# Gate and up products of a two-layer transformer trunk: high and low token parts in one 512-column matmul

## Chip, core and metric

The kernel runs on one core of one Trainium2 chip. The metric is the time of one execution on the device, in microseconds (us); less is better. Compared are medians of several runs.

## What is computed

Two layers over 256 tokens of width 1024. Each layer has a feed-forward part (swiglu), a mixer (two kinds of attention side by side) and a second feed-forward part, each between two RMS norms, with shifts, scales and gates worked out from a vector c. Cut to the part that matters here:

```python
D_MODEL, SEQ, DEPTH = 1024, 256, 2
D_FF = 2816

def swiglu(h, w_gate, w_up, w_down):
    return (jax.nn.silu(h @ w_gate) * (h @ w_up)) @ w_down

for l in range(DEPTH):
    mod = (c_act @ ada_w[l] + ada_b[l])[:, None, :]
    sh1, sc1, g1, sh2, sc2, g2, sh3, sc3, g3 = jnp.split(mod, N_MOD, axis=-1)
    h = rmsnorm(x, norm_pre[l, 0]) * (1.0 + sc1) + sh1
    y = swiglu(h, ffn_w_gate[l, 0], ffn_w_up[l, 0], ffn_w_down[l, 0])
    x = x + 0.5 * g1 * rmsnorm(y, norm_post[l, 0])
    ...  # the mixer, then the second swiglu with sh3, sc3, g3
```

All inputs and outputs are float32.

## The kernel before

**Precision.** TensorE multiplies in float32r, a form of float32 that keeps fewer bits. Every weight and every activation is therefore split into a high and a low part (`hi`, `lo`; for the tokens `hTh`, `hTl`), and a product is the sum of three matmuls: high by high, high by low, low by high. For weights ACT writes the high part (line 442) and DVE subtracts it from the raw data to get the low part (line 443), in pieces of 512 or 256 columns (function `unit`, `split` in the table SEC). A weight block is 128 x 2048 elements, 1 MB.

**The feed-forward part** (`ffn`, four calls). Its 2816 hidden columns are taken in 512 columns for each half of the tokens (`rows_of`, weights as the moving operand), and nine blocks of 256 columns (`j` = 0 to 8) for all 256 tokens at once, with the weights as the stationary operand. In a block, gate and up each have two column groups (`t`) of 128 hidden columns. A group is a sum over 8 steps of the inner dimension; `mm3t` runs its three matmuls (lines 489 to 491), each with 256 moving columns, the tokens of both halves. Gate fills one PSUM bank (two groups of 256), up another: `pair = (wps(), wps())`. Then `swiglu` (lines 634 to 638) takes Silu of the gate on ACT (636) and its product with up on DVE (637), both from PSUM; `split` writes the high and the low part of the result (630, 631). These activations are the stationary operand of the down products (`mm3`, lines 481 to 483, 512 columns), which add into four banks over the whole call. `mm3t` is also used in the mixer, in `cols_of` (line 726).

**Tiles and buffers.** `wps` gives a PSUM bank, of two pools (`w0`, `w1`) with two banks each; without an argument the pool goes by the block's parity. The other four banks hold the down sums. `st` gives SBUF tiles of 128 x 512 of two pools with three each. Raw weights have 3 buffers, high parts 6, low parts 5. So a weight load on SP's queue (line 431) waits until DVE has made the low part of an older block.

**Background work.** The shifts and scales of later parts are computed beside: SP loads pieces of `ada_w` (line 514), DVE multiplies and adds them (line 506, `acc`), and two matmuls (523, 524) sum over the partitions.

**The order of the work** is not that of the code. `keep_order` collects all instructions, takes a cost for each, runs a list schedule forward and backward five times, with due times, buffers and the constants of SEC, and fixes the resulting order on every engine. Any change in the instructions makes a new order everywhere.

Of the kernel before, what the change touches and what calls it, by code (L numbers as in the profile page):

```python
# [11 lines left out]
F32R = mybir.dt.float32r  # L12
# [283 lines left out]
def trunk(ctx, tc, x, c, rel_bias, ada_w, ada_b, norm_pre, norm_post, w_gate, w_up,  # L296
# [48 lines left out]
    def wps(h=None):  # L345
        return psw.tile([P, 512], F32, tag=f"w{cur[0] if h is None else h}", name=nm("w"))
# [7 lines left out]
    def ctile(shape, name, dt=F32):  # L354
        return cp.tile(shape, dt, tag=name, name=name)
# [104 lines left out]
    def u_both(l, f, w, tag, j):  # L460

        c0 = 512 + j * 256
        return unit((tag, l, f, "j", j), (8, 256), rows(w[l, f], 0, 8)[:, :, c0:c0 + 256])
# [14 lines left out]
    def mm3(ps_, hh, hl, wt, wk, sl, start, stop):  # L478
# [3 lines left out]
        nc.tensor.matmul(ps_, hh, wl, start=False, stop=False)  # L482
        nc.tensor.matmul(ps_, hl, wh, start=False, stop=stop)  # L483

    def mm3t(ps_, kt, wt, sl, start, stop):

        wh, wl = wt[0][:, kt, sl], wt[1][:, kt, sl]
        hh, hl = hT[0][:, :, kt, :], hT[1][:, :, kt, :]
        nc.tensor.matmul(ps_, wh, hh, start=start, stop=False)  # L489
        nc.tensor.matmul(ps_, wh, hl, start=False, stop=False)  # L490
        nc.tensor.matmul(ps_, wl, hh, start=False, stop=stop)  # L491
# [87 lines left out]
        nc.gpsimd.tensor_tensor(r2, r, mhalf, op=ALU.pow)  # L579
        return r2  # L580

    hT = [ctile([P, 2, KT, P], f"hT{n}", F32R) for n in "hl"]

    def to_T(h, k0, nk, src):

# [70 lines left out]
    def ffn(l, i, first):  # L656
        f = i // 2
        acts = []
        for h in range(2):
            cur[0] = h  # L660
            pair = first[h] if first else (wps(), wps())
            if not first:
                rows_of(h, pair, [lambda q: u_solo(l, f, w_gate, "g", q), lambda q: u_solo(l, f, w_up, "u", q)])
            acts.append(hidden_solo(pair))
        accs = [(aps(h), aps(h)) for h in range(2)]
        blocks = [[(acts[h], t * P) for t in range(4)] for h in range(2)]

        def down(h, u):

            w = u_down(l, f, u)  # L670
            for n in range(2):
                for k in range(2):
                    (hh, hl), c0 = blocks[h][u * 2 + k]
                    mm3(accs[h][n], hh[:, c0:c0 + P], hl[:, c0:c0 + P], w, k, slice(n * 512, (n + 1) * 512),
                        u == 0 and k == 0, u == 10 and k == 1)

        nd = 0
        for j in range(9):
            cur[0] = j % 2
            if first and j == SETUP:  # L680
                with shift(START_SMALL):
                    setup_table(*small)
                setup_bias()
            pair = (wps(), wps())
            for p_, (tag, ws) in zip(pair, (("g", w_gate), ("u", w_up))):
                w = u_both(l, f, ws, tag, j)
                for t in range(2):
                    for k in range(KT):
                        mm3t(p_[:, t * 256:(t + 1) * 256], k, w, slice(t * P, (t + 1) * P), k == 0, k == KT - 1)
            act = split(swiglu(*pair), 512)  # L690
            for h in range(2):
                blocks[h] += [(act, t * 256 + h * P) for t in range(2)]
            while nd < min(j + 2 - sec["lag"], 11 - sec["tail"]):
                for h in range(2):
                    down(h, nd)
                nd += 1
        for h in range(2):
            cur[0] = h
            for u in range(nd, 11):
                down(h, u)  # L700
            post_norm(h, l, i, accs[h])
            if (l, i) != (DEPTH - 1, 2):
                pre_norm(h, *((l, 1) if i == 0 else (l + 1, 0)))
# [340 lines left out]
```

## Time and profile before

| | |
|---|---|
| median of 3 runs | 1026.07 us (1024.99 to 1028.37) |
| the profiled execution | 1029.76 us, its span 1027.6 us |
| PE busy | 1007.1 us (98%), 6514 matmuls and as many weight loads |
| DVE busy | 800.6 us (78%) |
| ACT busy | 552.9 us (54%) |
| mean granted TensorE clock | 0.996 |
| moved by DMA | 265.10 MB |

PE is TensorE with its matmuls, PEld its weight loads, DVE is VectorE, ACT is ScalarE, SP issues the DMAs. The span is the time from the first to the last instruction. A matmul's duration is longer than the distance to the next one, since they are pipelined; the distance between two starts tells what one costs. In the names of tiles `_a` and `_b` stand for the parity of the block (or the half of the tokens), and the arrow points from what is read to what is written.

### The profile page before, as it was taken

The page shows a single profiled execution, that of the slowest core. Times are in us where ns is not written, and L with a number is a line of the kernel's source. Part 1 is how long each engine was busy: PE and PEld are TensorE (multiplying, and loading weights), DVE is VectorE, ACT ScalarE, POOL GpSimd, SP SyncE. Part 2 cuts the span into 40 slices and gives each one's busy share as a digit, 9 for nine tenths or more (in the row PEclk, how much of TensorE's full clock was granted, in tenths as well). Part 3 has the DMA queues.
Part 4 walks back from the last instruction along what each step waited for, and adds up shares of the span by engine and source line. Part 5 has one row for each costly group of instructions (what it writes and reads, how often), then busy time and mean ns, then how long its engine had stood idle before and what let it go on. Part 6 is the DMA issues. An engine that isn't in the chain of part 4 may idle for free. (4 is left out here: it accounts for less than half of the span.)

```text
span 1027.6 us, 17311 instructions
## 1 busy us (share of the span) xinstructions
PE 1007.1 (98%) x6514; PEld 895.9 (87%) x6514; DVE 800.6 (78%) x1493; ACT 552.9 (54%) x1250; POOL 41.3 (4%) x80
## 2 busy tenths in 40 slices
PE   8999998999999999999999999999999999999997
PEld 3699998988897899999979999998788879999996
DVE  4799886988997998798879887886879788555542
ACT  2456433574877665555465544545478666444431
POOL 1000000010001000000010000000100110000000
PEclk9999999999999999999999999999999999999999
DMA  9999999977895588899838988886589638655511
GB/s 327 364 343 340 315 290 342 331 251 251 308 321 203 196 278 294 280 317 312 282 133 290 319 273 276 301 291 242 160 295 330 207 125 274 200 175 195 183 64 41
DMA packets 173919, 265.10 MB, mean 258 GB/s; under 512 B 6412, under 2 KB 109548, under 8 KB 173836
## 3 DMA queue, kind: packets, MB, share of 16 engines
q1 hardware_dynamic: 173680, 263.93, 75.7%
q8 instruction: 51, 0.84, 0.3%
q14 instruction: 32, 0.26, 0.1%
q10 hardware_dynamic: 156, 0.07, 0.0%
HBM read 262.90 MB, written 4.22 MB: 260 GB/s over the span
## 5 line engine op out<-in xcount | busy, mean ns | idle before, releaser
L443 DVE TENSOR_TENSOR lo_a<-raw_a,hi_a 128x512 fp32r<-128x512 f32 (+1 forms) x540 | 293.6, 593 | 48.5 <-issue 24.2
L442 ACT ACTIVATE hi_a<-raw_a 128x512 fp32r<-128x512 f32 (+1 forms) x540 | 259.2, 547 | 121.2 <-DMA raw_a<-in_ffn_w_up_dram 28.3
L489 PE MATMUL w_a<-hTh,hi_a 128*128 128x256 f32 x768 | 219.6, 286 | 3.4 <-ACT hi_a L442 3.4
L490 PE MATMUL w_a<-hTl,hi_a 128*128 128x256 f32 x768 | 218.5, 285 | 0.0
L491 PE MATMUL w_a<-hTh,lo_a 128*128 128x256 f32 x768 | 217.7, 284 | 0.0
L489 PEld LDWEIGHTS w_a<-hTh,hi_a 128*128 128x128 f32 x768 | 147.7, 193 | 5.0 <-ACT hi_a L442 3.6
L490 PEld LDWEIGHTS w_a<-hTl,hi_a 128*128 128x128 f32 x768 | 147.9, 193 | 1.2 <-issue 0.3
L491 PEld LDWEIGHTS w_a<-hTh,lo_a 128*128 128x128 f32 x768 | 147.7, 192 | 0.4
L490 PE MATMUL w_b<-hTl,hi_b 128*128 128x256 f32 x512 | 144.8, 283 | 0.0
L489 PE MATMUL w_b<-hTh,hi_b 128*128 128x256 f32 x512 | 144.7, 283 | 0.0
L491 PE MATMUL w_b<-hTh,lo_b 128*128 128x256 f32 x512 | 144.6, 283 | 0.0
L443 DVE TENSOR_TENSOR lo_b<-raw_b,hi_b 128x512 fp32r<-128x512 f32 (+1 forms) x224 | 119.8, 589 | 24.6 <-issue 17.1
L442 ACT ACTIVATE hi_b<-raw_b 128x512 fp32r<-128x512 f32 (+1 forms) x224 | 105.3, 544 | 62.4 <-DMA raw_b<-in_ffn_w_up_dram 17.5
L489 PEld LDWEIGHTS w_b<-hTh,hi_b 128*128 128x128 f32 x512 | 98.1, 192 | 1.0
L490 PEld LDWEIGHTS w_b<-hTl,hi_b 128*128 128x128 f32 x512 | 98.1, 192 | 0.9
L491 PEld LDWEIGHTS w_b<-hTh,lo_b 128*128 128x128 f32 x512 | 98.0, 192 | 0.3
L506 DVE SCALAR_TENSOR_TENSOR acc_a<-araw_a,ccol,acc_a 128x512 f32<-128x512 f32 x110 | 82.2, 747 | 12.0 <-DMA araw_a<-in_ada_w_dram 10.6
L482 PE MATMUL a_b<-lo_a,str_a 128*128 128x512 f32 x156 | 60.8, 392 | 0.0
L483 PE MATMUL a_b<-hi_a,str_a 128*128 128x512 f32 x156 | 60.2, 390 | 0.0
L481 PE MATMUL a_b<-hi_a,str_a 128*128 128x512 f32 x156 | 59.7, 391 | 0.0
L506 DVE SCALAR_TENSOR_TENSOR acc_b<-araw_b,ccol,acc_b 128x512 f32<-128x512 f32 x46 | 34.5, 749 | 4.7 <-DMA araw_b<-in_ada_w_dram 3.9
L481 PE MATMUL w_a<-hi_a,hTh 128*128 128x512 f32 (+1 forms) x96 | 36.2, 378 | 0.6 <-DVE hTl L591 0.6
(245 smaller groups left out, 1724.1 us busy)
## 6 DMA issues: line engine op xcount, KB each, us to landing
araw_a<-in_ada_w_dram SPq DMA_DIRECT2D x84, 512.0 KB
raw_a<-in_ffn_w_down_dram SPq DMA_DIRECT2D x30, 1024.0 KB
raw_a<-in_ffn_w_gate_dram SPq DMA_DIRECT2D x26, 1024.0 KB
raw_a<-in_ffn_w_up_dram SPq DMA_DIRECT2D x26, 1024.0 KB
araw_b<-in_ada_w_dram SPq DMA_DIRECT2D x44, 512.0 KB
raw_a<-in_mix_w_in_dram SPq DMA_DIRECT2D x18, 1024.0 KB
raw_b<-in_ffn_w_gate_dram SPq DMA_DIRECT2D x16, 1024.0 KB
raw_b<-in_ffn_w_up_dram SPq DMA_DIRECT2D x16, 1024.0 KB
```

Of the source, the lines that this page charges most:

```text
L442: nc.scalar.activation(hi[:, sl], raw[:, sl], AF.Copy)
L443: nc.vector.tensor_sub(lo[:, sl], raw[:, sl], hi[:, sl].bitcast(F32))
L481: nc.tensor.matmul(ps_, hh, wh, start=start, stop=False)
L482: nc.tensor.matmul(ps_, hh, wl, start=False, stop=False)
L483: nc.tensor.matmul(ps_, hl, wh, start=False, stop=stop)
L489: nc.tensor.matmul(ps_, wh, hh, start=start, stop=False)
L490: nc.tensor.matmul(ps_, wh, hl, start=False, stop=False)
L491: nc.tensor.matmul(ps_, wl, hh, start=False, stop=stop)
L506: nc.vector.scalar_tensor_tensor(acc[:, :n], raw[:, t, :], ccol[:, k:k + 1], b if t == 0 else acc[:, :n], op0=ALU.mult, op1=ALU.add)
```

## The change

High and low part of the tokens now lie in one tile, `hTa[p, half, part, step, token]`. In the nine blocks of each feed-forward call a new function `mm2t` runs two matmuls for each step: the high weights against 512 columns (high part of both halves, then low part of both halves), and the low weights against the 256 columns of the high part. Columns 0 to 255 of the bank get high by high and low by high, columns 256 to 511 get high by low. So a column group fills a bank of its own: gate's two groups take the two banks of pool w0, up's those of w1. After a group ACT copies columns 256 to 511 to SBUF and DVE adds columns 0 to 255 to them. Silu and the product of gate and up then work in SBUF, in place. The mixer keeps `mm3t`. The tables of the planner are as they were.

```diff
+    def mm2t(ps_, k, wt, sl):
+        for kt in range(k):
+            wh, wl = wt[0][:, kt, sl], wt[1][:, kt, sl]
+            both = lambda **f: nc.tensor.matmul(ps_, wh, hTa[:, :, :, kt, :].rearrange("p h n t -> p n h t"), **f)
+            if kt < k - 1:
+                both(start=kt == 0, stop=False)
+            nc.tensor.matmul(ps_[:, :256], wl, hT[0][:, :, kt, :], start=False, stop=False)
+            if kt == k - 1:
+                both(start=kt == 0, stop=True)
...
-    hT = [ctile([P, 2, KT, P], f"hT{n}", F32R) for n in "hl"]
+    hTa = ctile([P, 2, 2, KT, P], "hT", F32R)
+    hT = [hTa[:, :, n] for n in range(2)]
...
-            pair = (wps(), wps())
-            for p_, (tag, ws) in zip(pair, (("g", w_gate), ("u", w_up))):
+            gu = []
+            for b, (tag, ws) in enumerate((("g", w_gate), ("u", w_up))):
                 w = u_both(l, f, ws, tag, j)
+                gu.append(st())
                 for t in range(2):
-                    for k in range(KT):
-                        mm3t(p_[:, t * 256:(t + 1) * 256], k, w, slice(t * P, (t + 1) * P), k == 0, k == KT - 1)
-            act = split(swiglu(*pair), 512)
+                    p_ = wps(b)
+                    mm2t(p_, KT, w, slice(t * P, (t + 1) * P))
+                    dst = gu[b][:, t * 256:(t + 1) * 256]
+                    nc.scalar.activation(dst, p_[:, 256:], AF.Copy)
+                    nc.vector.tensor_add(dst, p_[:, :256], dst)
+            nc.scalar.activation(gu[0], gu[0], AF.Silu)
+            nc.vector.tensor_mul(gu[0], gu[0], gu[1])
+            act = split(gu[0], 512)
```

The new order shows it at three places. The first is PE in the third block of the second feed-forward call, before (lines 489 to 491 are `mm3t`):

```order
L489 MATMUL w_a_4400<-hTh,hi_a_4475 128x256
L490 MATMUL w_a_4400<-hTl,hi_a_4475 128x256
L491 MATMUL w_a_4400<-hTh,lo_a_4476 128x256
L489 MATMUL w_a_4400<-hTh,hi_a_4475 128x256
L490 MATMUL w_a_4400<-hTl,hi_a_4475 128x256
L491 MATMUL w_a_4400<-hTh,lo_a_4476 128x256
```

And PE at the same place after (490 is the wide matmul, 493 the narrow one):

```order
L490 MATMUL w_a_4181<-hT,hi_a_4158 128x512
L493 MATMUL w_a_4181<-hT,lo_a_4159 128x256
L490 MATMUL w_a_4181<-hT,hi_a_4158 128x512
L493 MATMUL w_a_4181<-hT,lo_a_4159 128x256
L490 MATMUL w_a_4181<-hT,hi_a_4158 128x512
```

Three matmuls a step have become two, and the two read the same tile `hT`.

The second place is DVE at that block, before (637 is the product of gate and up, 443 a low part of weights, 506 a background sum):

```order
L443 TENSOR_TENSOR lo_b_4606<-raw_b_4603,hi_b_4605 128x256
L506 SCALAR_TENSOR_TENSOR acc_b_4634<-araw_b_4640,ccol,acc_b_4634 128x512
L506 SCALAR_TENSOR_TENSOR acc_b_4634<-araw_b_4712,ccol,acc_b_4634 128x512 x2
L443 TENSOR_TENSOR lo_b_4695<-raw_b_4692,hi_b_4694 128x256 x8
L637 TENSOR_TENSOR st_a_4546<-st_a_4545,w_a_4400 128x512
```

And DVE there after (707 is the new add, 709 the product, 518 a background sum):

```order
L443 TENSOR_TENSOR lo_b_4419<-raw_b_4416,hi_b_4418 128x256 x3
L707 TENSOR_TENSOR st_a_4180<-w_a_4181,st_a_4180 128x256
L443 TENSOR_TENSOR lo_b_4419<-raw_b_4416,hi_b_4418 128x256 x5
L518 SCALAR_TENSOR_TENSOR acc_b_4126<-araw_a_4239,ccol,acc_b_4126 128x512
L707 TENSOR_TENSOR st_a_4180<-w_a_4200,st_a_4180 128x256
L518 SCALAR_TENSOR_TENSOR acc_b_4126<-araw_a_4308,ccol,acc_b_4126 128x512 x2
L443 TENSOR_TENSOR lo_b_4488<-raw_b_4485,hi_b_4487 128x256 x2
L534 TENSOR_TENSOR ast_b_4359<-acc_b_4126,ast_b_4358 128x512
L707 TENSOR_TENSOR st_a_4243<-w_a_4244,st_a_4243 128x256
L443 TENSOR_TENSOR lo_b_4488<-raw_b_4485,hi_b_4487 128x256 x3
L707 TENSOR_TENSOR st_a_4243<-w_a_4263,st_a_4243 128x256
L709 TENSOR_TENSOR st_a_4180<-st_a_4180,st_a_4243 128x512
```

DVE has four adds in a block now, one for each column group, among the low parts of later weights.

The third place is PE in the first feed-forward call, at its third block, before (481 to 483 are down products):

```order
L482 MATMUL a_b_537<-lo_b_855,str_b_530 128x512
L483 MATMUL a_b_537<-hi_b_854,str_b_531 128x512
L489 MATMUL w_a_903<-hTh,hi_a_907 128x256
L490 MATMUL w_a_903<-hTl,hi_a_907 128x256
L491 MATMUL w_a_903<-hTh,lo_a_908 128x256
```

And there after:

```order
L482 MATMUL a_b_536<-lo_b_810,str_b_529 128x512
L483 MATMUL a_b_536<-hi_b_809,str_b_530 128x512
L490 MATMUL w_a_898<-hT,hi_a_860 128x512
L490 MATMUL w_a_934<-hT,hi_a_919 128x512
L490 MATMUL w_a_953<-hT,hi_a_919 128x512
L493 MATMUL w_a_879<-hT,lo_a_861 128x256
L490 MATMUL w_a_879<-hT,hi_a_860 128x512
L493 MATMUL w_a_879<-hT,lo_a_861 128x256
L490 MATMUL w_a_879<-hT,hi_a_860 128x512
L493 MATMUL w_a_898<-hT,lo_a_861 128x256
```

Where the block ran group by group, its four banks are now opened by single wide matmuls, before the low part of the weights is asked for.

## Rows read from the trace of the kernel before

**Rows 1.** Page, busy time (share, instructions) and 40 slices in tenths

```profile
PE 1007.1 (98%) x6514; PEld 895.9 (87%) x6514; DVE 800.6 (78%) x1493; ACT 552.9 (54%) x1250; POOL 41.3 (4%) x80
...
PEclk9999999999999999999999999999999999999999
```

**Rows 2.** Windows: from:to, length, busy us (instructions), clock, DMA share, GB/s

```profile
45.00:225.00 180.00, 176.61 (x1182) 163.13 (x1181) 155.82 (x246) 91.66 (x175) 1.63 (x4) 0.99 0.96 329
225.00:345.00 120.00, 117.83 (x714) 100.22 (x713) 104.14 (x230) 86.22 (x227) 14.09 (x24) 1.00 0.71 241
350.00:500.00 150.00, 150.00 (x1050) 140.88 (x1049) 132.29 (x308) 87.12 (x252) 0.00 (x0) 1.00 0.87 296
550.00:725.00 175.00, 174.60 (x1194) 162.37 (x1192) 141.21 (x222) 87.51 (x165) 5.06 (x8) 1.00 0.81 278
725.00:835.00 110.00, 107.47 (x648) 90.94 (x648) 92.03 (x199) 74.38 (x189) 9.32 (x16) 1.00 0.73 239
850.00:1000.00 150.00, 150.00 (x1071) 141.93 (x1071) 85.32 (x137) 70.62 (x130) 0.00 (x0) 1.00 0.54 183
...
375.00:400.00 25.00, 25.00 (x153) 22.41 (x152) 23.34 (x55) 13.27 (x41) 0.00 (x0) 1.00 0.90 305
```

**Rows 3.** PE's waits, the longest: us in total, times, longest

```profile
PE w_a L489 <- ACT hi_a L442: 3.4, 1, 3.4
```

**Rows 4.** Timeline of PE, a block product: start, duration, engine, line, operation

```profile
970.90 0.28 PE L489 MATMUL w_b<-hTh,hi_b 128*128 128x256 f32 x1
...
982.29 0.28 PE L491 MATMUL w_b<-hTh,lo_b 128*128 128x256 f32 x1
```

**Rows 5.** Timeline of PE, down products

```profile
505.90 0.40 PE L481 MATMUL a_b<-hi_a,str_b 128*128 128x512 f32 x1
...
522.93 0.39 PE L481 MATMUL a_b<-hi_a,str_b 128*128 128x512 f32 x1
```

**Rows 6.** Page, costliest groups: count, busy us, mean ns, idle before

```profile
L489 PE MATMUL w_a<-hTh,hi_a 128*128 128x256 f32 x768 | 219.6, 286 | 3.4 <-ACT hi_a L442 3.4
L489 PE MATMUL w_b<-hTh,hi_b 128*128 128x256 f32 x512 | 144.7, 283 | 0.0
```

**Rows 7.** Timeline of PE, mixer products with 256 columns in one piece

```profile
229.99 0.28 PE L482 MATMUL w_a<-lo_a,hTh 128*128 128x256 f32 x1
...
232.14 0.28 PE L482 MATMUL w_a<-lo_a,hTh 128*128 128x256 f32 x1
```

**Rows 8.** Groups of DVE and ACT by form, columns as in rows 6

```profile
L968 DVE TENSOR_TENSOR st_a<-st_a,w_a 128x256 f32<-128x256 f32 x4 | 1.7, 421 | 0.1
L637 DVE TENSOR_TENSOR st_a<-st_a,w_a 128x512 f32<-128x512 f32 x23 | 15.7, 685 | 15.7 <-PE w_a L491 14.8 <-PE w_a L483 0.7
L637 DVE TENSOR_TENSOR st_b<-st_b,w_b 128x512 f32<-128x512 f32 x19 | 13.0, 683 | 10.6 <-PE w_b L491 9.7 <-PE w_b L483 0.9
L606 DVE TENSOR_TENSOR st_a<-x,row_a 128x512 f32<-128x512 f32 x6 | 3.9, 685 | 0.0
L506 DVE SCALAR_TENSOR_TENSOR acc_a<-araw_a,ccol,acc_a 128x512 f32<-128x512 f32 x110 | 82.2, 747 | 12.0 <-DMA araw_a<-in_ada_w_dram 10.6
L590 ACT ACTIVATE hTh<-w_a 128x256 fp32r<-128x256 f32 x4 | 1.5, 384 | 12.3 <-PE w_a L588 12.3
```

**Rows 9.** Waits of SP's queue: us in total, times, longest

```profile
SPq L431 <- DVE lo_a L443: 311.4, 102, 13.3
SPq L431 <- DVE lo_b L443: 137.0, 44, 7.1
```

**Rows 10.** Timeline of PE and windows around its long wait

```profile
162.26 0.28 PE L490 MATMUL w_a<-hTl,hi_a 128*128 128x256 f32 x1
165.93 0.39 PE L489 MATMUL w_a<-hTh,hi_a 128*128 128x256 f32 x1 [3.39 <-ACT hi_a L442]
...
162.00:166.00 4.00, 0.61 (x6) 0.41 (x4) 0.09 (x1) 0.76 (x2) 0.00 (x0) 1.00 1.04 403
166.00:175.00 9.00, 9.00 (x63) 9.00 (x64) 8.02 (x13) 5.47 (x11) 0.00 (x0) 0.81 0.98 339
```

## Prediction, made before the changed kernel had run

> **What bounds the kernel now.** I read the page's busy table and slices first [rows 1]. PE is busy 98% of the span, and its clock line reads 9 throughout. DVE comes next with 78%, ACT with 54%. That is a mean over unlike stages, so I then read the window table by stage [rows 2]. The four feed-forward stages (here 45 to 225, 350 to 500, 550 to 725 and 850 to 1000 us) show PE busy 176.61 of 180, 150 of 150, 174.60 of 175 and 150 of 150 us; only the two mixers and the start show PE waiting. A busy PE need not be a PE at its best, so the third view is PE's waits [rows 3]: the longest is one of 3.4 us, for the high part of one weight block. In the feed-forward stages the end is therefore set by how many matmuls PE has to run and how far apart they start.
>
> **What a matmul costs.** In the product of one block, 96 matmuls of 256 columns start between 970.90 and 982.29 us [rows 4]: 11.39 us over 95 steps, 119.9 ns from start to start. The down products run 76 matmuls of 512 columns between 505.90 and 522.93 us [rows 5]: 17.03 us over 75 steps, 227.1 ns. The line through both is 0.419 ns for a column and 12.7 ns for a matmul whatever its width (227.1 - 119.9 = 107.2 ns for 256 more columns; 119.9 - 107.2 = 12.7). Each matmul has its own weight load in both stretches, so the 12.7 ns is for the pair.
>
> **The change part by part.**
> *Products.* Lines 489 to 491 run 768 and 512 times each [rows 6], 1280 times; 2 layers x 4 calls x 2 halves x 8 steps = 128 of these are the mixer's cols_of, which stays. In 1152 steps, three matmuls of 256 columns (3 x 119.9 = 359.7 ns) become one of 512 and one of 256 (227.1 + 119.9 = 347.0 ns). The step loses 12.7 ns and one weight load; 1152 x 12.7 ns = 14.6 us, 3.7 us in each of four feed-forward stages. The columns that move through PE stay the same.
>
> *The form of the wide operand.* The 512 columns are four pieces of 128 with two different distances between them, which no matmul of the trace has. Nearest rows: 256 columns in two pieces start 119.9 ns apart [rows 4], and 256 columns in one piece, between 229.99 and 232.14 us, 2.15 us over 18 steps, 119.4 ns [rows 7]. A break costs 0 to 0.5 ns. At the other end, a 512-column matmul that is worth no more than two of 256 would cost 239.8 ns and save nothing. I take 227.1, since the row for breaks is the nearer one; three breaks at 0.5 ns would take 1.7 us of the 14.6.
>
> For the 12.7 ns, the trace and the Trainium skill differ. The Trainium skill (TensorE: Matmul & The Clock Gate, section "Wait — 56ns, not 53.3ns?") puts the fixed part of a warm matmul at about 2.5 ns, measured on bf16; by it the 1152 removed matmuls would be worth an estimated 2.9 us. The rows disagree; they are of this kernel's float32r products, and the sum goes by them.
>
> *Work added behind PE.* Each of the 144 column groups now leaves its bank through an ACT copy and a DVE add of 128x256. The same kinds of instruction stand in the trace: an ACT copy from PSUM of 128x256 with 384 ns, a DVE tensor_tensor of 128x256 with one PSUM operand with 421 ns [rows 8]. The Silu and the product of the gate are as many as before; they read SBUF now, which for a DVE product of 128x512 makes no difference (685 ns at line 606 as at line 637) [rows 8]. So a feed-forward stage gets 36 x 0.384 = 13.8 us of ACT and 36 x 0.421 = 15.2 us of DVE. ACT has room everywhere (87.12 busy of 150 us in the second stage). DVE idles 24.2, 17.7, 33.8 and 64.7 us in the four windows [rows 2]. The second is the tight one: 17.7 us less the 3.7 that the stage gets shorter leaves 14.0 for 15.2. What makes it fit is the order: between the first and the last block product of that stage DVE had 52 of the background sums of line 506 and has 47 now (the first stage 56 and 49, the third 55 and 40), and five of them are 5 x 0.747 = 3.7 us [rows 8]. They go to the stretches between stages; DVE is at 87% and 84% in the mixers' windows. I count this at nothing and give it a rival.
>
> *The wait that is new.* The first wide matmul of a group now waits until the DVE add has emptied the bank's last holder; behind it on PE stands everything. After a group ends the chain is a copy and an add, 0.384 + 0.421 us, and the same bank is wanted only three groups later, 3 x 8 x 347 ns = 8.3 us. Nothing is paid as long as the add is not kept behind other work for over 7 us.
>
> *The tail of a block.* From its last matmul to the split, a block went through Silu and product and now goes through copy, add, Silu and product, 0.8 us more. The down products take their activation a block or more later, and 96 down matmuls (21.8 us at 227.1 ns) follow the last block in both orders. Nothing.
>
> *Order and queues.* The planner orders everything anew. In the first stage it now opens the four banks of a block with single wide matmuls ahead of their low weights; in the last it alternates wide and narrow. The queue of SP has the same 421 rows in a changed order. Weight loads are issued when the low split of an older block frees its buffer: SP's longest waits are for line 443 on DVE, 311.4 and 137.0 us in all [rows 9]. So DVE's lateness travels by the DMA queue to the next weights.
>
> **How much of 14.6 us arrives.** The second, third and fourth stage have PE at 100% and DMA engines at 0.87, 0.81 and 0.54 [rows 2]. I count their 3 x 3.7 = 11.0 us in full. The first has DMA at 0.96 over 180 us, and PE's one long wait lies in it: after 162.26 us the next matmul starts at 165.93, waiting for a high part, with the DMA engines at 1.04 meanwhile, and over the next 9 us the granted clock is 0.81 on average, so part of them went at the lower of its two levels [rows 10]. A PE that arrives there earlier waits longer. I count nothing for the first stage. The mixers I count as they were: their order changes in places, with no sign that I can read.
>
> Sum: -11.0 us. The profiled execution took 1029.76 us, with a span of 1027.6; less 11.0 that is 1018.8 and a span of 1016.6. This execution lay 3.7 us above the median of 1026.07, so the median should be **1015** us.
>
> **The rivals.**
> *All of it and the long wait too.* If the new order brings the block of 162 us in time, the first stage gains its 3.7 us, the gap of 3.6 us closes, and the 9 us at 0.81 give back 1.7: 1026.1 - 14.6 - 3.6 - 1.7 = 1006 us. For it: the gap is one event, and the loads around it are reordered. Against it: DMA at its limit.
>
> *DVE fills up in the second stage.* Then the 3.7 us of that stage go too, and, as the background sums moved between the stages, up to 4 us of the gains there: 1026.1 - 7.3 = 1018.8, with the sums 1023. For it: 14.0 us of room for 15.2 us of adds, and SP waiting for DVE. Against it: windows of 25 us with DVE 93% busy (23.34 of 25) keep PE busy for all 25 [rows 2].
>
> *No gain in the product.* The wide matmul at 239.8 ns, because its four pieces are fetched as two: 1026. A fixed part far below 12.7 ns would come out nearly there. The rule of the Trainium skill named above would give an estimated 1023 to 1024. Against both stand two straight stretches of rows.
>
> *The adds wait at the head of DVE's queue: slower.* The products of line 637 waited for PE 14.8 + 9.7 us [rows 8], over 42 of them 0.58 us each. If each add waits as long, it holds DVE 1.0 us, 36 us in a stage; less the background sums that left (7, 5 and 15 at 0.747 us), DVE is short of 6.6 us in the first stage and 14.6 in the second, has room in the others, and these gain 3.7 each: 21.2 - 7.4 = +13.8, 1040 us. It decides from the point where a wait of an add exceeds (17.7 + 3.7 - 15.2 - 3.7) / 36 = 0.07 us in the second stage and (24.2 + 5.2 - 15.2 - 3.7) / 36 = 0.29 us in the first; slower than before it gets from about 0.4 us. Against it: while DVE waits for PE, PE is the late one, and the low parts behind the add were made some blocks ahead.
>
> **How the numbers follow.** The forecast has 0.50, its own range 1010 to 1019 (the first stage's 3.7 us, the breaks, a little of the mixers). All of it and the wait 0.10, DVE filling up 0.20, no gain 0.08, slower 0.12. The range reaches from 1006 to 1025: it leaves out the slower case and half of no gain. What a measurement can tell from no change is about 0.3%, 3.1 us, so faster means under 1023: 0.50 + 0.10 + 0.20 = 0.80; same 0.08; slower 0.12.
>
> **What would show it.** In the changed profile: 1152 fewer matmuls and weight loads (5362); in a clean block, wide and narrow matmuls starting 227 and 120 ns apart, 347 ns a step (240 and 120 would be the third rival); 144 copies near 0.38 and 144 adds near 0.42 us; DVE over 90% in the second stage with PE still at 100%; the stretch from the first to the last block shorter by some 3.7 us in three stages and not in the first. Wrong would be: waits of PE for low parts in the second stage, DVE adds that wait long for PE while the split behind them is wanted, or mixers that grow by more than 3 us.

## Result and profile after

The changed kernel takes 1035.56 us (median of five runs; the kernel before in the same batch 1028.37): 1.0084 times the time, interval 1.0060 to 1.0107. That is slower, 20 us above the forecast and outside its range. One of the five executions took 1656.43 us at a mean granted clock of 0.557 and is left out of the ratio. The profiled execution took 1039.71 us with a span of 1037.9, against 1029.76 and 1027.6. So the two profiles lie 10 us apart and the medians 7; what is read from the profiles below is to be taken with these 3 us.

The first line of the profile page of the changed kernel (busy us, share, instructions) answers to [rows 1]:

```profile
PE 1003.7 (97%) x5362; PEld 835.5 (81%) x5362; DVE 848.1 (82%) x1637; ACT 599.0 (58%) x1394; POOL 40.8 (4%) x80
```

The 1152 matmuls and weight loads are gone. Yet PE is busy only 3.4 us less, and it is idle 34.2 us (1037.9 - 1003.7) where it was idle 20.5 (1027.6 - 1007.1). The windows of [rows 2], now of the changed kernel, show where:

```profile
45.00:225.00 180.00, 171.94 (x869) 142.58 (x868) 156.85 (x267) 97.83 (x198) 0.82 (x1) 0.98 0.91 306
225.00:345.00 120.00, 115.45 (x694) 97.48 (x693) 103.55 (x223) 84.07 (x221) 12.34 (x22) 0.99 0.77 260
350.00:500.00 150.00, 149.96 (x780) 127.54 (x779) 134.83 (x317) 92.01 (x261) 1.33 (x3) 1.00 0.78 263
550.00:725.00 175.00, 175.00 (x905) 149.09 (x905) 157.75 (x266) 97.03 (x195) 0.83 (x2) 1.00 0.88 301
725.00:835.00 110.00, 105.34 (x651) 89.73 (x650) 91.39 (x199) 73.21 (x188) 9.71 (x17) 1.00 0.75 248
850.00:1000.00 150.00, 149.85 (x784) 127.51 (x783) 106.83 (x183) 86.91 (x171) 1.21 (x2) 1.00 0.60 200
sum 885.00, PE 867.55 PEld 733.93 DVE 751.20 ACT 531.06 POOL 26.24; mean PE 144.59 PEld 122.32 DVE 125.20 ACT 88.51 POOL 4.37
```

PE idles 8.1 us in the first window (3.4 before), 4.6 and 4.7 in the two mixers' windows (2.2 and 2.5), and next to nothing in the other feed-forward stages. PE's longest waits in the changed kernel (us in total, times, longest), where [rows 3] had one of 3.4 us:

```profile
PE a_b L481 <- ACT hi_a L442: 5.9, 2, 5.5
PE w_a L481 <- DVE hT L605: 3.3, 1, 3.3
...
PE w_b L831 <- ACT st_b L825: 2.2, 1, 2.2
PE w_a L736 <- DVE st_a L781: 1.5, 1, 1.5
PE w_b L602 <- DVE st_b L859: 1.3, 1, 1.3
```

None of them is for a copy or an add of the change. L481 is a down product that waits for the high part of its weights, and then, at 541.29 us, the first product of the third feed-forward call, which starts when DVE has written the low part of the first tokens (L605). L831, L736 and L602 belong to the mixers and the norms. The wait at 541.29 shows what an order does:

```profile
537.63 1.07 ACT L604 ACTIVATE hT<-w_a 128x512 fp32r<-128x512 f32 x2
539.22 1.42 DVE L638 SCALAR_TENSOR_TENSOR x<-st_b,rstd_b,x 128x512 f32<-128x512 f32 x2 [0.24 <-POOL rstd_b L591]
540.55 0.68 DVE L605 TENSOR_TENSOR hT<-w_a,hT 128x512 fp32r<-128x512 f32 x1
541.29 0.50 PE L481 MATMUL w_a<-hi_a,hT 128*128 128x512 f32 x1 [3.34 <-DVE hT L605]
```

The high part, all that this product reads, was there at 538.70. DVE did the norm of the other half of the tokens (L638) ahead of L605. Whether PE waited for the joined tile `hT` or for the PSUM bank that L605 still had to read is not told apart; with two separate tiles, before, the same kind of product also waited once for the low part, 0.6 us (at 229.77). The longest wait, in the timeline of PE and of ACT and in windows (columns as in the windows above):

```profile
175.01 0.40 PE L536 MATMUL w_a<-ast_a,onesr 128*128 128x512 f32 x1
180.92 1.22 PE L481 MATMUL a_b<-hi_a,str_a 128*128 128x512 f32 x2 [5.52 <-ACT hi_a L442]
...
180.24 1.67 ACT L442 ACTIVATE hi_a<-raw_a 128x512 fp32r<-128x512 f32 x3 [5.08 <-DMA raw_a<-in_ffn_w_down_dram]
...
175.00:181.00 6.00, 0.48 (x3) 0.08 (x1) 1.39 (x3) 0.93 (x3) 0.00 (x0) 0.91 1.04 361
181.00:200.00 19.00, 19.00 (x86) 15.86 (x87) 14.87 (x25) 11.06 (x23) 0.00 (x0) 0.85 1.06 337
```

It is of the kind of the wait in [rows 10], 13 us later in the span and 2.1 us longer. PE waits for a conversion by ACT, ACT for a DMA, and the DMA engines are full. The granted clock is 0.85 over the 19 us behind it, so part of them went at the lower level.

**A ledger.** Add up, in each trace, what every matmul of the product functions (mm3, mm3t, mm2t) takes from its start to the next one's beyond 119.9 ns (256 columns) or 227.1 ns (512), and all the time of the other matmuls (transposes, attention, sums). Before this is 132.2 us, after it is 157.3. From before to after the last matmul's start moves by 1031.3 - 1021.0 = +10.3 us; that is -14.6 us for the merged matmuls at the forecast's price and +25.1 us of this sum (the rest is rounding). Of the 25.1, some 6 us are a spacing that the forecast had too small (below). The other 19 lie by stage: first feed-forward call 7.0, first mixer 4.4, the transition from the second call to the third 4.2, second mixer 1.6, start 1.6, the rest spread. By the first and last block product of each call, the third call went from 150.4 to 148.0 us and the fourth from 143.1 to 140.7, each 2.4 us shorter. The end of the first call came 3.4 us later; mixer, second call and transition together went from 339.8 to 349.7 us; the second mixer grew by 1.7. The second call itself, with the transition to the third, went from 192.6 to 195.0 us, though the forecast had its 3.7 us in full.

### The profile page after: what moved, and what is told of

The parts are those of the page before. It is cut to its first block, busy times and chain, and to the rows that moved or that the text cites. A ratio compares the mean times of both kernels' runs of the same rounds, so it can differ in the third digit from the quotient of the medians.

```text
span 1037.9 us, 15226 instructions
## 1 busy us (share of the span) xinstructions
PE 1003.7 (97%) x5362; PEld 835.5 (81%) x5362; DVE 848.1 (82%) x1637; ACT 599.0 (58%) x1394; POOL 40.8 (4%) x80
## 5 line engine op out<-in xcount | busy, mean ns | idle before, releaser
L490 PE MATMUL w_a<-hT,hi_a 128*128 128x512 f32 x640 | 223.9, 397 | 0.0
L490 PE MATMUL w_b<-hT,hi_b 128*128 128x512 f32 x512 | 179.4, 397 | 0.0
L493 PE MATMUL w_a<-hT,lo_a 128*128 128x256 f32 x640 | 166.8, 281 | 0.1
L490 PEld LDWEIGHTS w_a<-hT,hi_a 128*128 128x128 f32 x640 | 116.8, 188 | 22.4
L493 PE MATMUL w_b<-hT,lo_b 128*128 128x256 f32 x512 | 132.5, 281 | 0.0
L493 PEld LDWEIGHTS w_a<-hT,lo_a 128*128 128x128 f32 x640 | 120.7, 189 | 7.5 <-DVE lo_a L443 0.6
L490 PEld LDWEIGHTS w_b<-hT,hi_b 128*128 128x128 f32 x512 | 93.5, 188 | 18.1 <-ACT hi_b L442 0.2
L493 PEld LDWEIGHTS w_b<-hT,lo_b 128*128 128x128 f32 x512 | 96.5, 189 | 6.0
L518 DVE SCALAR_TENSOR_TENSOR acc_a<-araw_a,ccol,acc_a 128x512 f32<-128x512 f32 x110 | 82.1, 746 | 14.0 <-DMA araw_a<-in_ada_w_dram 12.7
L481 PE MATMUL a_b<-hi_a,str_a 128*128 128x512 f32 x156 | 60.7, 402 | 5.5 <-ACT hi_a L442 5.5
L707 DVE TENSOR_TENSOR st_a<-w_a,st_a 128x256 f32<-128x256 f32 x80 | 33.3, 420 | 21.7 <-ACT st_a L706 21.5
L481 PE MATMUL w_a<-hi_a,hT 128*128 128x512 f32 (+1 forms) x96 | 37.1, 386 | 3.3 <-DVE hT L605 3.3
L481 PEld LDWEIGHTS a_b<-hi_a,str_a 128*128 128x128 f32 x156 | 30.2, 194 | 11.9 <-ACT hi_a L442 6.0
```

The source lines that it names most:

```text
L481: nc.tensor.matmul(ps_, hh, wh, start=start, stop=False)
L490: both = lambda **f: nc.tensor.matmul(ps_, wh, hTa[:, :, :, kt, :].rearrange("p h n t -> p n h t"), **f)
L493: nc.tensor.matmul(ps_[:, :256], wl, hT[0][:, :, kt, :], start=False, stop=False)
L518: nc.vector.scalar_tensor_tensor(acc[:, :n], raw[:, t, :], ccol[:, k:k + 1], b if t == 0 else acc[:, :n], op0=ALU.mult, op1=ALU.add)
L707: nc.vector.tensor_add(dst, p_[:, :256], dst)
```

## Experiments

Two theories stand against each other. **The order** (O): the matmuls gain, but the planner writes every queue anew, with constants that were chosen for the old instructions, and the new order lets PE wait in stages where it does not set the end. **The added work** (B, and E for the adds alone): copies, adds and the banks that they hold cost the time in any order. A side question (P, Q) is why a step gained less than 12.7 ns. Ratios are to the kernel before in the same batch, with the interval.

**e1: the merge taken back, the rest kept.** Banks, copies and adds as in the change, three matmuls of 256 columns (those of the low token part ahead of the others), the order made anew (arguments shortened):

```
+  for kt in range(k): matmul(ps_[:, 256:], wt[0][:, kt, sl], hT[1][:, :, kt, :])
   for kt in range(k):
-      both(...)
+      matmul(ps_[:, :256], wh, hh)
       matmul(ps_[:, :256], wl, hh)
```

> The changed kernel with its wide matmul taken apart again: banks, copies and adds as changed, but high by low as 256-column matmuls of its own (first the eight of a group, then the pairs), 6514 matmuls. In the changed kernel's trace a wide matmul starts the next after 233 ns and a narrow one after 118, 351 ns a step, against 360 for three narrow ones. Theory O (the product gains, the new order of the work loses it): slower than the changed kernel by 1152 x 9 ns = 10 us, so about 1045 us. Rival P (the wide matmul saves nothing): the same as the changed kernel within 3 us, about 1035.

Measured: 1042.6 us, 1.0134 [1.0110, 1.0158]. That is 7 us above the change (5 by the ratios), nearer to theory O's 1045 than to P's 1035, and 14 us above the kernel before with as many matmuls. The merge gains; the loss is in the rest. The 7 us are not the merge's price alone, since the order is another one too.

**e2: no adds, the planner free.**

```
-  activation(dst, p_[:, 256:], Copy)
-  tensor_add(dst, p_[:, :256], dst)
+  activation(dst, p_[:, :256], Copy)
```

> The changed kernel without the 144 adds on DVE: ACT copies columns 0 to 255 of each bank, and the product of high weights with low tokens, which PE still computes, is left out of the result. Rival E (the adds themselves cost: DVE's 48 to 60 us of work and the waits at the head of its queue): falls by the whole loss, to about 1015. Theory O: the order is made anew without the adds, so some of the loss may go by chance, but PE's idle time in the mixers and the first stage (28 us more than before) stays for the larger part: 1025 to 1035.

Measured: 1023.94 us, 0.9957 [0.9940, 0.9974]. That is between the two forecasts. 11.6 us come back with the adds, but the planner also made another order: both theories can have this.

**e3 and e4: the planner's price of a matmul.** The planner prices a matmul by its columns with a small fixed part; here it gets the line of [rows 4, 5], in the changed kernel (e3) and in the kernel before (e4). No instruction is added or left out.

```
-  return max(free, 256) / 2.4 + 2.5
+  return free * 0.419 + 12.7
```

> The changed kernel, but the planner takes for a float32r matmul what the trace shows, 0.419 ns a column and 12.7 ns a matmul (227 ns for 512 columns, 120 for 256), where it had 216 and 109. Nothing else is changed: the same instructions in another order. Theory O: the idle time comes from the order, so another order moves the time by more than 3 us, and one made with true costs gets most of the gain: 1015 to 1022. Rival E: the work on DVE is the same, so within 4 us of the changed kernel, 1031 to 1039.

> The kernel before with the same true matmul costs in its planner: what another order alone does to it. Theory O in its strong form (the constants of the tables fit the order that before had, and any other order is worse): slower by 3 to 10 us, 1031 to 1038. In the weak form (true costs make a better order for either): 1015 to 1025. Rival E says nothing of it.

Measured: e3 1039.01 us, 1.0100 [1.0073, 1.0126]; e4 1051.2 us, 1.0233 [1.0204, 1.0262]. e3 is a miss for theory O: truer prices made no better order, and the time is at the upper end of rival E's range. Its longest wait of PE is for one of the new adds. The add stands on DVE behind four low parts and a background sum, and holds the bank into which PE is to sum over the partitions (L535). So the change does add waits that an order can run into:

```profile
PE w_b L535 <- DVE st_b L707: 5.1, 2, 4.7
```

e4 is the strongest single result on the order. The kernel before, with the same instructions in another sequence, is 22 us slower, more than the 3 to 10 us that were expected. Windows of e4:

```profile
45.00:225.00 180.00, 170.03 (x1143) 157.03 (x1142) 153.76 (x242) 85.90 (x160) 0.29 (x1) 0.97 0.97 327
225.00:345.00 120.00, 113.76 (x684) 95.96 (x684) 95.82 (x208) 77.75 (x205) 11.26 (x20) 1.00 0.73 241
350.00:500.00 150.00, 146.03 (x943) 133.09 (x942) 129.23 (x300) 86.06 (x249) 2.04 (x4) 0.99 0.82 273
...
725.00:835.00 110.00, 104.67 (x629) 88.79 (x628) 84.21 (x182) 68.38 (x174) 7.66 (x15) 0.98 0.74 238
```

It idles 10.0 us in the first window, 6.2 and 5.3 in the mixers and 4.0 in the second feed-forward stage: mostly the places at which the changed kernel lost, without any of the change.

**e5: small adds in the same order.** The add covers 7 of the 256 columns; the planner prices it as the full one, so that every queue keeps the changed kernel's order.

```
-  tensor_add(dst, p_[:, :256], dst)
+  tensor_add(dst[:, :7], p_[:, :7], dst[:, :7])
```

> The changed kernel with every instruction in its place on every queue (the planner still counts the adds as before), but each of the 144 adds on DVE touches 7 columns in place of 256, so the product of high weights with low tokens is left out of nearly all of the result. The 144 waits of DVE for ACT's copy stay; some 144 x 0.26 = 37 us of DVE work go. Theory O (the order loses the gain): within 4 us of the changed kernel, 1031 to 1037. Rival E (the adds' time on DVE loses it): 1020 to 1026.

Measured: 1035.03 us, 1.0073 [1.0061, 1.0086]. Groups of DVE in e5 (count, busy us, mean ns, idle before):

```profile
L709 DVE TENSOR_TENSOR st_a<-w_a,st_a 128x7 f32<-128x7 f32 x80 | 12.7, 162 | 30.4 <-ACT st_a L708 30.3
L709 DVE TENSOR_TENSOR st_b<-w_b,st_b 128x7 f32<-128x7 f32 x64 | 10.1, 162 | 24.7 <-ACT st_b L708 24.2
```

The adds went from 420 and 419 ns to 162, 37 us less of DVE, and the time by 0.5 us. In this order DVE's time isn't what is paid for.

**e6: the wide operand in one piece.** The wide matmul reads 512 neighbouring columns, all of the high part; the order is the same.

```
-  hTa[:, :, :, kt, :].rearrange("p h n t -> p n h t")
+  fl(hTa[:, 0, 0, 0:4, :])
```

> The changed kernel in the same order on every queue, but the wide matmul reads 512 columns that lie in one piece (the same ones at every step, so the results of the blocks are wrong numbers). In the changed kernel wide matmuls start the next after 233 ns, the down products' after 227. If the four pieces cost the 6 ns: a step of 347 ns, 1152 x 4 to 6 ns = 5 to 7 us faster than the changed kernel where PE is the limit, about 1029 to 1031. If they do not: the same as the changed kernel, 1033 to 1037, and 233 in the trace.

Measured: 1035.78 us, 1.0082 [1.0069, 1.0096]. The breaks in the operand cost nothing.

**e7: the change in the second layer's calls alone** (`if l == 1:` the new block, else the old one).

> The change in the third and the fourth feed-forward call alone; the first two use the old product. In the changed kernel those two stages were each 2.4 us shorter from first to last block matmul, the first was 1.8 us longer and the stretch between first and second 7.4 us longer. Theory O: the third and fourth give 4.8 us, and the order of the first layer is again a new one with chance gains or losses of some us: 1021 to 1030. Rival E: DVE has 34 and 65 us idle in these two stages, the adds fit: about 1024.

Measured: 1027.69 us, 0.9983 [0.9971, 0.9996]. The third and fourth call are 2.3 and 2.4 us shorter, as in the full change. Of these 4.7 us, 0.2 are left by the medians (1027.91 before in this batch) and 1.7 by the ratio. The first mixer, none of whose instructions the edit touches, grew from 147.2 to 151.9 us between the block products around it; PE is busy 114.12 us in its window, where it was 117.83 [rows 2]:

```profile
225.00:345.00 120.00, 114.12 (x692) 96.63 (x691) 100.94 (x222) 81.57 (x218) 11.14 (x21) 1.00 0.72 236
```

**e8: the changed kernel near the old order.** What is ready is ranked by its place in the order of the kernel before, in one pass of the planner:

```
-  best = forward(prio)
-  last = best
-  for _ in range(FBI):
...
+  best = forward(ranks_of_before)
```

> The changed kernel, its matmuls, copies and adds untouched, but the planner ranks what is ready by the place that the instruction had in the order of the kernel before (the wide matmul takes the place of the first of its two, the copy and the add stand at the end of their product). So each queue comes near the old order, but for what the new copies and adds and their banks force. Theory O (the loss of the change is that the planner fell into a worse order): the old order with 1152 steps that are 7 to 9 ns shorter, 1017 to 1024 us, ratio 0.990 to 0.997. Rival B (the loss is in what the change itself adds, the chain matmul, copy, add, bank free, whatever the order): 1033 to 1042 us, ratio 1.005 to 1.014.

Measured: 1034.87 us, 1.0072 [1.0047, 1.0096], as rival B had it: the old order is no cure. It says that the new instructions do not fit the old places; that they lose in any order is B's claim, and e11 below is against it. PE's longest waits in e8:

```profile
PE w_a L487 <- ACT hi_a L439: 5.0, 1, 5.0
PE w_a L599 <- DVE st_a L620: 3.4, 2, 3.0
...
PE w_a L490 <- DVE lo_a L440: 2.1, 1, 2.1
```

The second call was 1.6 us shorter than before this time, the third 1.4 and the fourth 2.4, and all of it and more was lost in the first call (166.1 us for 160.1) and the first mixer (153.3 for 147.2).

**e9: no adds, every queue in the order of the changed kernel.** The edit of e2, with the sequence on each engine written out as the changed kernel has it, less the 144 adds.

> The changed kernel without the 144 adds: the copy takes columns 0 to 255 of the bank, columns 256 to 511 (the product of the low token part with the high weights) are left out of the result. Unlike in e2_no_add, where the planner was free to make another order and the time was 1023.9 us, every queue here keeps the order of the changed kernel, the adds alone are missing, so that a bank is free after its copy. Theory O: with that order held the time stays at 1033 to 1036 us, ratio 1.005 to 1.009. Rival B (the chain over the add keeps banks, and so TensorE, waiting): the gain of e2_no_add comes back without a new order, 1023 to 1028 us, ratio 0.995 to 1.000.

Measured: 1032.52 us, 1.0044 [1.0028, 1.0061]. That is just below theory O's range and far from B's. Without the adds, 3 us come back in the sequence of the change (4 by the ratios) and 11.6 in a new one (e2): of e2's gain, 3 to 4 us are the adds and the banks that they hold, and the rest is the order.

**e10: runs of wide and narrow.** The order of every queue as in the change, but inside a product seven wide matmuls, eight narrow ones and the last wide one:

```
+  for kt in range(k - 1): both(kt)
+  for kt in range(k):     narrow(kt)
+  both(k - 1)
```

> The changed kernel with the same order on every queue, except that inside each of the 144 products the sixteen matmuls stand in another sequence: seven wide ones, eight narrow ones, the last wide one, instead of wide and narrow in turn. In the trace of the changed kernel a wide matmul has 227 ns to a wide one behind it, but 233 to 235 to a narrow one. Theory P (the pair of unlike matmuls costs the 5 ns, so that a step is 352 instead of the 347 ns of the prediction): steps come to 348 ns, 1152 x 4 to 5 ns = 4.6 to 5.8 us less, 1029 to 1031.5 us, ratio 1.002 to 1.005. Rival Q (a wide matmul of this operand is followed 233 ns later by whatever comes): nothing changes, 1034 to 1037 us, ratio 1.007 to 1.009.

Measured: 1032.12 us, 1.0043 [1.0026, 1.0059], between the two theories' ranges by its time and in P's by its ratio, 3.4 us less than the change. The timeline of PE, first of the changed kernel, then of e10 (start, duration of the group, operation, count):

```profile
967.15 0.40 PE L490 MATMUL w_a<-hT,hi_a 128*128 128x512 f32 x1
...
975.60 0.40 PE L490 MATMUL w_a<-hT,hi_a 128*128 128x512 f32 x1
```

```profile
960.97 2.00 PE L490 MATMUL w_a<-hT,hi_a 128*128 128x512 f32 x8
962.82 1.11 PE L495 MATMUL w_a<-hT,lo_a 128*128 128x256 f32 x8
963.77 2.00 PE L490 MATMUL w_a<-hT,hi_a 128*128 128x512 f32 x8
965.61 1.12 PE L495 MATMUL w_a<-hT,lo_a 128*128 128x256 f32 x8
966.56 0.40 PE L490 MATMUL w_a<-hT,hi_a 128*128 128x512 f32 x1
```

In turn, 24 steps take 8.45 us, 351.9 ns each; in runs, 16 steps take 5.59 us, 349.2 ns. By means over all products, a wide one has 234.3 ns to the next matmul and a narrow one 117.7 in the change, 229.8 and 119.0 in e10. P has its sign right, its size too large (4.6 to 5.8 us forecast), and its mechanism is not borne out: in e10 the step from wide to narrow itself has 227.7 ns, and in the change a wide one followed by another wide one has 234.2 (102 of them), where the expectation had 227. So it is not the single pair of unlike matmuls that costs; what does is open.

**e11 to e15: constants chosen anew.** The planner's offsets, shares and slacks (the numbers of SEC, START_..., FSLACK, BSLACK and BACKLOG) come from a random search that lowers the planner's own total, one for each kernel and meant to be about as long (the length is not on record). e11 is the changed kernel, e12 the kernel before as a control, e13 the change in the second layer with the runs of e10, e14 the change everywhere with the runs, e15 is e13 without the runs. A piece of the edit of e11:

```
-  dict(plan=('3542', 20, 3), tail=1, lag=1, split=4, sum=-921, dma=-218),
+  dict(plan=('3542', 18, 6), tail=2, lag=2, split=4, sum=-1564, dma=-2408),
...
-  START_MM, START_CONV, START_CHAIN, START_SMALL = 590, 826, -286, 74
+  START_MM, START_CONV, START_CHAIN, START_SMALL = 205, -720, -1390, 602
```

> The changed kernel with other constants of the planner (the offsets, shares and slacks that set where each stage's side work is started), searched anew for it; no instruction added or left out but that side work stands elsewhere. Theory O (the change gains 9 us in matmuls and loses them again in an order made with constants that were fitted to the old set of instructions): with fitted constants it falls below the kernel before, 1015 to 1025 us, ratio 0.988 to 0.998. Rival B (copies, adds and banks cost the time whatever the order): 1030 us or more, ratio 1.003 or more.

> The kernel before with constants of the planner searched anew in the same way and for about as long: the control for e11_change_retuned. Theory O (constants of before were fitted to it): little to find, 1022 to 1029 us, ratio 0.995 to 1.002, so that the changed kernel, fitted, beats it. Rival R (constants of before were as far from their best as those of the changed kernel): it gains as much as e11 does, ratio 0.985 to 0.993, and the change is worth nothing of its own.

> The change in the two feed-forward calls of the second layer alone, as in e7_second_layer (1027.7 us), with wide and narrow matmuls in runs as in e10_wide_then_narrow, and with constants searched anew for it. Theories O and P together: 576 steps gain 7 to 12 ns, 4 to 7 us, and the order no longer takes them back: 1015 to 1022 us, ratio 0.988 to 0.995, below both kernels. Rival B: 1026 to 1030 us, ratio 0.999 to 1.003.

> The change in all four feed-forward calls, wide and narrow matmuls in runs as in e10_wide_then_narrow, constants of the planner searched anew. Against e11_change_retuned (1022.1 us), if the sequence in a product is worth what e10 showed (3.4 us): 1017 to 1021 us, ratio 0.989 to 0.993. If the search had taken that gain already, or if it is lost in the stage that waits for DMA: 1021 to 1024 us, ratio 0.993 to 0.996.

> As e13_layer2_retuned (1017.3 us), but wide and narrow matmuls in turn as the change has them: the sequence alone is taken back, in 576 steps. By e10 (3.4 us over 1152 steps) it costs 1.5 to 3 us: 1018.5 to 1020.5 us, ratio 0.990 to 0.993. If the sequence costs nothing once the order is fitted: 1016.5 to 1018 us, ratio 0.988 to 0.990.

| kernel | us | ratio to before | span | PE busy | PE idle |
|---|---|---|---|---|---|
| before | 1028.37 (beside the change) | 1 | 1027.6 | 1007.1 | 20.5 |
| change | 1035.56 | 1.0084 [1.0060, 1.0107] | 1037.9 | 1003.7 | 34.2 |
| e4 before, other order | 1051.2 | 1.0233 [1.0204, 1.0262] | 1055.5 | 1015.1 | 40.4 |
| e11 change, new constants | 1022.05 | 0.9939 [0.9923, 0.9954] | 1021.4 | 997.5 | 23.9 |
| e12 before, new constants | 1024.02 | 0.9961 [0.9947, 0.9974] | 1024.3 | 1005.7 | 18.6 |
| e13 second layer, runs | 1017.26 | 0.9889 [0.9872, 0.9907] | 1015.7 | 998.5 | 17.2 |
| e14 all, runs | 1017.52 | 0.9899 [0.9882, 0.9915] | 1014.3 | 992.9 | 21.4 |
| e15 second layer, in turn | 1019.34 | 0.9913 [0.9896, 0.9929] | 1017.6 | 999.3 | 18.3 |

All five came out in expected ranges, e11, e12 and e13 in theory O's, e14 and e15 in those by which the sequence is worth what e10 showed. Span and busy times are those of one profiled execution each. The windows of the first stage and of the first mixer, of e11, then of e14:

```profile
45.00:225.00 180.00, 178.57 (x918) 149.71 (x917) 163.04 (x277) 104.03 (x211) 2.61 (x5) 1.00 0.87 296
225.00:345.00 120.00, 115.10 (x694) 98.87 (x692) 103.38 (x229) 85.07 (x225) 12.64 (x22) 0.99 0.83 275
```

```profile
45.00:225.00 180.00, 179.15 (x931) 151.61 (x930) 166.08 (x283) 105.54 (x219) 2.91 (x6) 1.00 0.90 302
225.00:345.00 120.00, 114.98 (x693) 97.60 (x692) 101.15 (x227) 82.93 (x221) 13.08 (x21) 1.00 0.80 266
```

The same instructions as in the change, in another sequence, take 13.5 us less (e11). PE idles 1.4 us in the first window instead of 8.1, with the granted clock at 1.00 there. PE's busy time fell by 6.2 us too, with no matmul gone: a PE that waits less also runs less at the lower clock, which by the mean granted clocks (0.993 and 0.997) makes some 4 of these 6.2 us. Against the control, the change in turn is worth 2.0 us (1024.02 to 1022.05; the intervals of the two ratios overlap) and with the runs 6.5 us (e14). In the second layer alone it is worth 4.7 us in turn and 6.8 with the runs. 576 steps at 359.7 - 351.9 = 7.8 ns make 4.5 us, and at 359.7 - 349.2 = 10.5 ns they make 6.0: there the gain arrives in full. The traces agree: from the first block product of the third call to the last matmul e12 has 468.0 us, e11 463.9, e15 462.4, e13 459.0 and e14 459.3, the last two some 3 us below what the matmuls account for.

In the time as a whole the first layer's calls add nothing to it (e14 against e13). e13 and e14 beat both kernels, and the control. The second call does gain: with the transition to the third it has 192.6 us before and in e12, 189.6 in e11 and 189.1 in e14. What is lost lies ahead of it: its first block starts at 357.0 us in e12, 361.3 in e11 and 359.3 in e14. What stays open is how near to their best these orders are (one search each), and so whether the first call and the first mixer must lose or no sequence was found in which they do not. The DMA engines, at 0.96 in the first window before [rows 2], do not explain it: in e11 and e14 PE idles 1.4 and 0.9 us in that window. It is the first mixer's window that loses some 5 us of PE there, where e12 and e13 lose 1.5 and 1.6.

## Why the prediction failed

**The sign failed at one step: "The mixers I count as they were: their order changes in places, with no sign that I can read."** A new order was given the price of nothing, and no rival had a loss by it as its mechanism. The runs put a price on it. With the same instructions, the order moved the kernel before by +22 us (e4) and -4 (e12), and the changed kernel by +3.5 (e3) and -13.5 (e11). In the profiled executions the changed kernel has 14 us more of PE's idle time, and a lower clock behind the long waits; the adds and their banks are 3 to 4 us of the loss (e9). The code had a clue: the constants of the planner are given stage by stage, to the last digit, as if fitted to one set of instructions (which is not shown; e12 found 4 us there too); a few instructions more in each of 36 blocks move the side work of every stage. A price could have been bounded from the rows: PE's idle time, 20.5 us, was what that order had left, and there was no reason for the next one to leave as little.

**The second call was counted in full and gave nothing.** Its window had PE at 100%, before and after, and with the transition to the third call it still became 2.4 us longer (192.6 to 195.0). With new constants it is 3.0 and 3.5 us shorter (e11, e14). A full window said that PE bounds the stage, and not that the stage's ends would stay as they were.

**The slower rival had the wrong mechanism.** It gave 1040 us by adds that wait at the head of DVE's queue. The adds did wait, 36.4 us for their copies:

```profile
DVE st_a L707 <- ACT st_a L706: 21.5, 26, 2.4
DVE st_b L707 <- ACT st_b L706: 14.9, 19, 1.8
```

But DVE had the time, and e5 took 37 us of it away for 0.5 us. DVE filling up in the second stage falls with it: DVE is at 134.83 of 150 us there and PE at 149.96, as the prediction's main line had it. The background sums between the first and the last block product are by the traces 54 before and 46 after in the second call, where the prediction had 52 and 47, and 60 and 54 in the third, where it had 55 and 40.

**The step was mis-sized.** 359.7 to 347.0 ns was forecast, 12.7 ns; in the changed kernel a step takes 351.9, so it gains 7.8 ns, 9.0 us in 1152 steps instead of 14.6. Both prices were taken from stretches of one width (227.1 and 119.9 ns); with widths in turn the wide one has 234.3 ns to the narrow one behind it and the narrow one 117.7 to the next wide one. The bound at the other end, 239.8, was not far off for the wide one. The Trainium skill (TensorE: Matmul & The Clock Gate, section "Wait — 56ns, not 53.3ns?") with its fixed part of some 2.5 ns would have given 2.9 us, an estimate; the measured 9.0 lies between it and the forecast's 14.6.

**Counted right.** 5362 matmuls; copies and adds at their price, 379 and 420 ns by the groups of the changed kernel's page:

```profile
L706 ACT ACTIVATE st_a<-w_a 128x256 f32<-128x256 f32 x80 | 30.2, 379 | 65.5 <-PE w_a L490 65.3
...
L707 DVE TENSOR_TENSOR st_a<-w_a,st_a 128x256 f32<-128x256 f32 x80 | 33.3, 420 | 21.7 <-ACT st_a L706 21.5
```

The adds cost no time of DVE that PE would have to wait for (e5); together with the banks that they hold they cost 3 to 4 us in the order of the change (e9). For the banks the prediction had nothing to pay, as the next block wants one only 8.3 us later; the background sums want banks too, and in e3 one of them makes PE wait 4.7 us for an add. The copies on ACT were not taken out by any run; e11, e13 and e14 have copies and adds, and none of them is slower than the control. The first call gave nothing back, as forecast, and in fact took 1.8 us more. The third and fourth call each became 2.4 us shorter, the forecast's 3.7 at the smaller step. "Wrong would be ... mixers that grow by more than 3 us" was the sign that came: the first mixer grew by 7.4 us from the last block of the first call to the first block of the second.

## What to carry over

Where a planner or hand-set constants make the order of all queues, a change of the instructions is also a draw of a new order; price that first (here up to 22 us, against 9 us in the matmuls), and compare only kernels whose constants were chosen with the same effort, the kernel before among them. Cost a matmul by the sequence in which it will stand and not by a stretch of its own width; put equal widths in runs. Ask of every stage by itself whether it keeps a gain in PE's work: here the second layer kept it, the second call too once the constants were chosen anew, and the first call with its mixer did not, for a reason that no run shows; so the change in the second layer alone (e13) was as fast as the change everywhere (e14).

## What the hardware showed that was not expected

- **Widths in turn are dearer than widths in runs.** Wide and narrow in turn, 351.9 ns a step; in runs, 349.2; by the prices of the down products and of the old blocks it would be 347.0. What makes the difference is not shown; it is not the four pieces (e6).
- **A wait of PE is paid twice.** After 5.5 us without a matmul the granted clock was 0.85 over the next 19 us, after 3.3 us (at 541.29) it was 0.80 over 8.7 us, and before the change after 3.4 us it was 0.81 over 9 us [rows 10]. e11, whose longest wait is 3.5 us, has a mean granted clock of 0.997 instead of 0.993 and 6.2 us less of busy time for the same instructions.
